# One-bank PSUM tiles in place of two-bank tiles for the last two token tiles of a decoder trunk

## The chip, the cores and the metric

The kernel runs on one core of a Trainium2 chip. The metric is device time in microseconds (us), the median of several runs. The core has five engines that work side by side, each through its own queue in order: TensorE (PE) for matmuls, VectorE (DVE) and ScalarE (ACT) for elementwise work, GpSimd (POOL), and SyncE (SP), which here only issues transfers. PE writes its results to PSUM, which is handed out in eight banks of 128 partitions by 512 float32 values. The profile shows loads of stationary operands as a row of their own (PEld).

## The reference

The model is a residual stream `x` of 512 tokens by 1024 features that passes through two layers, an attention mixer (MLA) and a gated linear attention (GLA), each followed by a squared-ReLU MLP, and a last RMSNorm. The part that matters here is the end:

```python
def sq_relu_mlp(xn, w_up, w_down):
    hid = jnp.square(jax.nn.relu(xn @ w_up))
    return hid @ w_down

for i in range(DEPTH):
    ...
    x = x + sq_relu_mlp(rms_norm(x, norm_mlp[i]), mlp_w_up[i], mlp_w_down[i])
return rms_norm(x, final_norm)
```

## The kernel before, in words

The stream is kept transposed: `xT[m]`, m = 0 to 7, is a tile of 128 features by 512 tokens. Every float32 product is done as three matmuls on parts (`mm3`, lines 110 to 112: high times high, high times low, low times high).

The MLP (`mlp`) goes over the 4096 hidden features in eight blocks of 512. `up` or `up_fast` computes a block `hid`; `down` multiplies it by its rows of `w_down` and adds the result to `xT` (line 787). `up_fast` runs seven products into two-bank PSUM tiles "z" and "y" (lines 879 and 880) and interleaves them with the `down` tiles of the block before.

The last block of the last layer is done by `down_final` instead, because the final norm follows at once. Its two halves of the tokens take different ways:

- Tokens 0 to 255 stay transposed. For m = 0 to 7 a bank "b" takes 12 matmuls of 256 columns, line 809 adds it to `xT[m]`, and `Final.add` collects squares and scaled copies. `Final.mean` (lines 1433 and 1434) sums the squares on PE, `Final.finish` computes the root on ACT and DVE, scales the eight copies (line 1443) and sends them out in four transfers (line 1444).
- Tokens 256 to 511 are two token-major tiles, t = 2 and t = 3, of 128 tokens by 1024 features. Each is two column halves, c = 0 and c = 1, and each half fills one bank with 12 matmuls of 512 columns. For t = 2 the residual is transposed by PE into a bank "b" (line 127), copied by ACT (line 824) and added by DVE (line 825). For t = 3 PE adds the residual itself, by four matmuls with the identity (line 831). `Final.row` then squares the half on ACT (line 1455), multiplies it by the gain on DVE (line 1456), and after c = 1 computes the row factor (lines 121, 1464 to 1466), scales the row (lines 1470 and 1472) and sends it out (line 1473).

PSUM is divided by `psum_layout`, which closes the current pool of tiles and opens another. There are two layouts:

```python
BANKS = {False: {"a": 2, "b": 3, "c": 3}, True: {"b": 3, "c": 1}}
```

With True, the remaining four banks are the two tiles "z" and "y", each 128 by 1024, so two banks and one tile (`two_banks`); `split_banks` returns the two halves of such a tile. Before the change `down_final` runs under True, and t = 2 takes the halves of "z", t = 3 those of "y".

The order of the work is not written out by hand. The program is traced in the order of the source, and a planner places each instruction on its engine's queue: by the order of the source, but where the next instruction would have to wait by the planner's reckoning, a later one that is ready goes ahead. It also sets the waits: an instruction that writes a tile waits for those that still read what was there, and the first instruction on a bank after a pool is closed waits for the last use of that bank in the old pool (`reuse_waits="tile"`: tile by tile).

Of the kernel before, what the change touches and what calls it, by code (L numbers as in the profile page):

```python
# [48 lines left out]
def trunk_kernel(ctx: ExitStack, tc: tile.TileContext, t_in: dict, out: bass.AP, out_row: bass.AP):  # L49
# [7 lines left out]
    def uname(s):  # L57
        count[0] += 1
        return f"{s}_{count[0]}"
# [5 lines left out]
    def psum_layout(paired):  # L65
        if psum:
            psum["es"].close()
        es = psum["es"] = ExitStack()
        psum["pool"] = es.enter_context(
            tc.tile_pool(name=uname("psum"), bufs=1, space=bass.MemoryType.PSUM, reuse_waits="tile")  # L70
        )
        psum["banks"] = BANKS[paired]

    def bank(tag):
        return psum["pool"].tile([P, 512], F32, tag=f"ps_{tag}", bufs=psum["banks"][tag], name=uname("ps"))

    def two_banks(tag):
        return psum["pool"].tile([P, 1024], F32, tag=f"ps_{tag}", bufs=1, name=uname("ps2"))

    def split_banks(tag):  # L80
        t = two_banks(tag)
        return [t[:, :512], t[:, 512:]]
# [4 lines left out]
    def tmp(shape=(P, 512), dt=F32):  # L87
        return sb.tile(list(shape), dt, tag="tmp", bufs=6, name=uname("tmp"))
# [5 lines left out]
    def both_parts():  # L94
        return sb.tile([P, 2, S], F32R, tag="set_A", bufs=8, name=uname("set"))
# [4 lines left out]
    def split(src, hi, lo, hi_eng=ACT, lo_eng=DVE, order=lambda i: i):  # L100
        if hi_eng is ACT:
            order(ACT.activation(hi, src, AF.Copy))  # L102
        else:
            hi_eng.tensor_copy(hi, src)
        lo_eng.tensor_tensor(lo, src, f(hi), ALU.subtract)  # L105

    def mm3(psum, w, x, start, stop):
        wh, wl = w
        xh, xl = x
        PE.matmul(psum, wh, xh, start=start, stop=False)  # L110
        PE.matmul(psum, wh, xl, start=False, stop=False)  # L111
        PE.matmul(psum, wl, xh, start=False, stop=stop)  # L112
# [13 lines left out]
    def tr(psum, src):  # L126
        PE.transpose(psum, src, ident[: src.shape[0], : src.shape[0]])  # L127


    def load(src, a, n):  # L130
        raw = sb.tile([P, a, n], F32, tag="wraw", bufs=2, name=uname("wraw"))
        SP.dma_start(raw, src)
        return raw
# [7 lines left out]
    def cut(pair, *idx):  # L141
        return tuple(t[idx] for t in pair)
# [601 lines left out]
    def mlp(layer, nrm, tag, nxt, final=False):  # L744
# [28 lines left out]
        def down(b, hid):  # L773
            for c in range(2):
                src = w_dn[b * FB : (b + 1) * FB, c * 512 : (c + 1) * 512].rearrange("(k p) n -> p k n", p=P)
                if c == 0 and b < NB - 1:
                    raw = fast.tile([P, 4, 512], F32, tag="raw", name=uname("raw"))
                    SP.dma_start(raw, src)
                else:
                    raw = load(src, 4, 512)  # L780
                for g in range(2):
                    w = piece(raw[:, :, g * 256 : (g + 1) * 256], 4, 256)
                    for j in range(2):
                        m = c * 4 + g * 2 + j
                        p = bank("b")
                        a_type(p, w, hid, cols=slice(j * P, (j + 1) * P))
                        DVE.tensor_tensor(xT[m], p, xT[m], ALU.add)  # L787
                        if b == NB - 1:
                            nxt.add(m, xT[m])
                        yield  # L790
# [3 lines left out]
        def down_final(b, hid):  # L794
            W = []
            for c in range(2):
                raw = load(
                    w_dn[b * FB : (b + 1) * FB, c * 512 : (c + 1) * 512].rearrange("(k p) n -> p k n", p=P), 4, 512
                )
                for k in range(4):  # L800
                    w = both_parts()
                    split(raw[:, k], w[:, 0], w[:, 1])
                    W.append((w[:, 0], w[:, 1]))
            for m in range(ND):
                p = bank("b")[:, :TH]
                for k in range(4):
                    w = cut(W[m // 4 * 4 + k], slice(None), slice(m % 4 * P, (m % 4 + 1) * P))
                    mm3(p, w, cut(hid[k], slice(None), slice(0, TH)), k == 0, k == 3)
                DVE.tensor_tensor(xT[m][:, :TH], p, xT[m][:, :TH], ALU.add)
                nxt.add(m)  # L810
            for t in (2, 3):
                tk = slice(t * P, (t + 1) * P)
                ps_ = split_banks("zy"[t % 2])
                for c in range(2):
                    for k in range(4):
                        mm3(ps_[c], cut(hid[k], slice(None), tk), W[c * 4 + k], k == 0, t == 2 and k == 3)
                        if t == 2 and c == 0 and k == 1:
                            nxt.mean()
                    if t == 2:
                        x_t = bank("b")  # L820
                        for j in range(4):
                            tr(x_t[:, j * P : (j + 1) * P], xT[c * 4 + j][:, tk])
                        y = tmp()
                        ACT.activation(y, x_t, AF.Copy)
                        DVE.tensor_tensor(y, ps_[c], y, ALU.add)
                        nxt.row(t, c, y)
                        if c == 0:
                            nxt.finish()
                    else:
                        for j in range(4):  # L830
                            PE.matmul(ps_[c][:, j * P : (j + 1) * P], xT[c * 4 + j][:, tk], ident, start=False, stop=j == 3)
                        nxt.row(t, c, ps_[c])
# [110 lines left out]
        for b in range(NB):  # L943
            if b + 1 < NB:
                tiles = down(b, hid)

                def others(n):
                    for _ in range(n):
                        next(tiles)

                hid = up_fast(b + 1, others)
                continue
            es.close()
            if final:
                down_final(b, hid)
            else:
                for _ in down(b, hid):
                    pass
# [440 lines left out]
    n_mix1 = Norm(ND, inv_d, "mix", ND)  # L1399
    psum_layout(True)  # L1400
    mlp(0, n_mlp0, "B", n_mix1)
    psum_layout(False)
    Y = gla(0, n_mix1, "B", "B")
# [71 lines left out]
    fin = Final()  # L1475
    psum_layout(True)
    mlp(1, n_mlp1, "B", fin, True)
    fin.es.close()

# [49 lines left out]
```

## Time and profile before

| | |
|---|---|
| median of 3 runs | 1104.48 us (1103.9 to 1104.51) |
| the profiled execution | 1105.92 us |
| its span, first to last instruction | 1103.5 us |
| mean granted TensorE clock | 0.995 |
| busy: PE, PEld, DVE, ACT, POOL | 99%, 83%, 78%, 50%, 4% of the span |
| PE's share of the chain that ended last | 96% |

The span is what the profile covers; the time of the execution includes about 2.4 us around it. A row of the instructions in order of time has the start in us, the duration in us, the engine, the line of the source, the operation, its output and inputs by tile names, and the shapes; "x8" merges eight instructions into one row, and a bracket at the end gives the idle time of the engine before it and the engine and line that ended it. In the list of waits, a row has who waited, for whom, the total in us, how often, and the longest. Matmuls of PE overlap: the pace is read from the starts, not from the durations.

### The profile page before, as it was taken

To read this page: it belongs to the slowest core of one execution; us is meant where nothing else is said; L and a number is where in the kernel's file an instruction comes from. 1 tells how busy PE (TensorE), PEld (TensorE's weight loads), DVE (VectorE), ACT (ScalarE), POOL (GpSimd) and SP (SyncE) were. 2 spreads that over 40 slices of the span, in tenths; PEclk is the share of its full clock that TensorE was granted. 3 is DMA by queue.
4 is the path that set the end of the run, shared out by engine and by line. 5 is a ranking of instruction groups with operands and counts; after the bars stand their busy time and mean duration, and the time that the engine had idled before them with its cause. 6 is when DMAs were issued, how large, how long until landed. Compare 5 with 4: busy or idle time off the path is not lost.

```text
span 1103.5 us, 14105 instructions
## 1 busy us (share of the span) xinstructions
PE 1090.2 (99%) x5428; PEld 918.9 (83%) x5428; DVE 856.4 (78%) x1417; ACT 546.3 (50%) x907; POOL 40.1 (4%) x72
## 2 busy tenths in 40 slices
PE   9999999999999999999999999999999999999996
PEld 7788888888888888888788888888888888888895
DVE  7789867987977977977596584478888788788773
ACT  7576654553453454454345735455444444445452
POOL 7210002000000000000000000000000000000000
PEclk9999999999999999999999999999999999999998
DMA  7312123142332332322312222232233233233122
GB/s 221 77 48 77 39 77 115 60 133 77 103 127 77 102 127 77 100 92 82 96 62 77 78 77 77 77 115 77 77 115 114 77 116 114 77 115 115 39 96 76
DMA packets 85987, 101.35 MB, mean 92 GB/s; under 512 B 7360, under 2 KB 63936, under 8 KB 85920
## 3 DMA queue, kind: packets, MB, share of 16 engines
q1 hardware_dynamic: 84112, 99.40, 28.4%
q10 hardware_dynamic: 1808, 1.05, 0.4%
q8 instruction: 42, 0.69, 0.3%
q14 instruction: 25, 0.20, 0.1%
HBM read 98.35 MB, written 2.10 MB: 91 GB/s over the span
## 4 chain that ended last, share of the span: by engine, by line
PE 96%; DVE 1%; ACT 1%; DMA 1%; issue 0%; ACTq 0%; DVEq 0%
PE ps L110 21%; PE ps L111 21%; PE ps L112 21%; PE ps L879 16%; PE ps L880 8%; PE ps L127 2%; PE ps L1155 1%; DMA wraw_ckv<-in_mla_w_in_dram 1%; PE ps L630 0%; PE ps L1226 0%; PE ps L631 0%; PE ps L629 0%; PE ps L628 0%; PE ps L627 0%; PE ps L1205 0%; DMA xT<-in_x_dram 0%
## 5 line engine op out<-in xcount | busy, mean ns | idle before, releaser
L110 PE MATMUL ps<-set,wh 128*128 128x512 f32 x776 | 304.7, 393 | 0.2 <-ACT set L237 0.2
L111 PE MATMUL ps<-set,wh 128*128 128x512 f32 x776 | 303.2, 391 | 0.8 <-DVE set L238 0.8
L112 PE MATMUL ps<-set,wl 128*128 128x512 f32 x776 | 302.8, 390 | 0.0
L102 ACT ACTIVATE wh<-wraw 128x1024 fp32r<-128x1024 f32 x139 | 147.0, 1060 | 242.0 <-PE ps L111 122.1
L105 DVE TENSOR_TENSOR wl<-wraw,wh 128x1024 fp32r<-128x1024 f32 x139 | 170.2, 1225 | 41.0 <-ACT wh L102 41.0
L110 PEld LDWEIGHTS ps<-set,wh 128*128 128x128 f32 x776 | 145.8, 188 | 31.8 <-ACT set L237 0.9
L111 PEld LDWEIGHTS ps<-set,wh 128*128 128x128 f32 x776 | 146.0, 188 | 31.4 <-DVE set L238 2.0
L112 PEld LDWEIGHTS ps<-set,wl 128*128 128x128 f32 x776 | 145.8, 188 | 30.6
L879 PE MATMUL ps<-T,wh 128*128 128x512 f32 x448 | 157.5, 391 | 0.0
L880 PE MATMUL ps<-T,wl 128*128 128x256 f32 x448 | 126.2, 282 | 0.0
L879 PE MATMUL ps<-set,wh 128*128 128x512 f32 x336 | 119.9, 397 | 0.0
L879 PEld LDWEIGHTS ps<-T,wh 128*128 128x128 f32 x448 | 84.1, 188 | 18.2
L880 PE MATMUL ps<-set,wl 128*128 128x256 f32 x336 | 94.2, 280 | 0.0
L105 DVE TENSOR_TENSOR wl<-comb,wh 128x1024 fp32r<-128x1024 f32 x42 | 51.4, 1224 | 47.2 <-ACT wh L102 46.9
L787 DVE TENSOR_TENSOR xT<-ps,xT 128x512 f32<-128x512 f32 x120 | 82.4, 687 | 6.7 <-PE ps L112 6.7
L102 ACT ACTIVATE wh<-comb 128x1024 fp32r<-128x1024 f32 x42 | 44.6, 1061 | 83.3 <-PE ps L879 80.0
L880 PEld LDWEIGHTS ps<-T,wl 128*128 128x128 f32 x448 | 84.6, 189 | 0.5
L879 PEld LDWEIGHTS ps<-set,wh 128*128 128x128 f32 x336 | 63.1, 188 | 15.1
L897 DVE TENSOR_TENSOR tmp<-ps,tmp 128x512 f32<-128x512 f32 x98 | 67.3, 686 | 1.0
L880 PEld LDWEIGHTS ps<-set,wl 128*128 128x128 f32 x336 | 63.4, 189 | 1.6
L110 PE MATMUL ps<-wh,set 128*128 128x512 f32 x144 | 59.6, 414 | 0.0
L102 ACT ACTIVATE wh<-raw 128x1024 fp32r<-128x1024 f32 x28 | 29.5, 1054 | 57.9 <-PE ps L879 55.1
(351 smaller groups left out, 1658.3 us busy)
## 6 DMA issues: line engine op xcount, KB each, us to landing
wraw<-in_mlp_w_up_dram SPq DMA_DIRECT2D x32, 1024.0 KB, 5.4
wraw<-in_mlp_w_down_dram SPq DMA_DIRECT2D x18, 1024.0 KB, 5.1
raw<-in_mlp_w_down_dram SPq DMA_DIRECT2D x14, 1024.0 KB, 5.1
wraw<-in_gla_w_in_dram SPq DMA_DIRECT2D x12, 1024.0 KB, 5.2
wraw<-in_mla_w_o_dram SPq DMA_DIRECT2D x4, 1024.0 KB, 5.0
wraw<-in_gla_w_o_dram SPq DMA_DIRECT2D x4, 1024.0 KB, 5.0
xT<-in_x_dram SPq DMA_DIRECT2D x6, 256.0 KB, 6.5
wraw<-in_mla_w_in_dram SPq DMA_DIRECT2D x3, 512.0 KB, 7.4
```

What stands on the lines that cost most here:

```text
L102: order(ACT.activation(hi, src, AF.Copy))
L105: lo_eng.tensor_tensor(lo, src, f(hi), ALU.subtract)
L110: PE.matmul(psum, wh, xh, start=start, stop=False)
L111: PE.matmul(psum, wh, xl, start=False, stop=False)
L112: PE.matmul(psum, wl, xh, start=False, stop=stop)
L127: PE.transpose(psum, src, ident[: src.shape[0], : src.shape[0]])
L787: DVE.tensor_tensor(xT[m], p, xT[m], ALU.add)
L879: PE.matmul(o.rearrange("p (h t) -> p h t", h=2), wh, x, start=start and k == 0, stop=False, skip_group_check=True)
L880: PE.matmul(o[:, :TH], wl, x[:, 0], start=False, stop=k == KH - 1, skip_group_check=True)
L897: DVE.tensor_tensor(by_tile(r), high, by_tile(r), ALU.add)
L1155: PE.matmul(p[:, t - t0], k[:, t * P : (t + 1) * P], moving[:, t], start=True, stop=True)
```

## The change

Each of the two token-major tiles takes two one-bank tiles, of tag "a" for t = 2 and of tag "c" for t = 3, in place of one two-bank tile. For that, PSUM is switched to the layout with a, b and c before `down_final`; there the b banks of the loop over m, of `Final.mean` and of the transposes come from the new pool as well. The number and the shape of all instructions stay the same.

```diff
             for t in (2, 3):
                 tk = slice(t * P, (t + 1) * P)
-                ps_ = split_banks("zy"[t % 2])
+                ps_ = [bank("ac"[t % 2]) for _ in range(2)]
                 for c in range(2):
                     for k in range(4):
                         mm3(ps_[c], cut(hid[k], slice(None), tk), W[c * 4 + k], k == 0, t == 2 and k == 3)
...
             es.close()
             if final:
+                psum_layout(False)
                 down_final(b, hid)
```

## The prediction

> **What bounds the kernel now.** I read the page's span first, then the list of what TensorE (PE) waited for over the whole run, then the waits of the last 44 us, then the two stretches around the longest one, and last the instructions in order of time.
>
> ```profile
> span 1103.5 us, 14105 instructions
> ```
>
> ```profile
> PE ps L110 <- DVE sm L1459: 3.8, 1, 3.8
> PE ps L1366 <- DVE ones L165: 1.2, 1, 1.2
> PE ps L111 <- DVE set L238: 0.8, 1, 0.8
> PE ps L630 <- ACT set L610: 0.3, 1, 0.3
> PE ps L110 <- ACT set L237: 0.2, 1, 0.2
> ```
>
> ```profile
> PEld ps L110 <- DVE tmp L825: 0.3, 1, 0.3
> PEld ps L110 <- DVE xT L787: 0.2, 1, 0.2
> ```
>
> The second fence is everything that PE waited for in 1103.5 us: it is the bound nearly everywhere, and more than half of its 6.3 us of named idle time is one wait, on VectorE (DVE), in front of a `mm3` matmul. The third fence holds two short waits of the weight loads in the same last part. So a change that only touches the final block can give about what that one wait costs, and the rest of the working is its price.
>
> ```profile
> 1085.65:1090.55 4.90, 1.05 (x10) 0.86 (x8) 4.33 (x12) 2.21 (x7) 0.00 (x0) 0.87 0.62 214
> 1090.55:1097.03 6.48, 6.47 (x20) 5.13 (x20) 0.01 (x1) 0.00 (x0) 0.00 (x0) 0.57 0.21 81
> ```
>
> ```profile
> 1084.97 0.39 PE L110 MATMUL ps<-set,set 128*128 128x512 f32 x1
> 1085.19 0.39 PE L111 MATMUL ps<-set,set 128*128 128x512 f32 x1
> 1085.42 0.39 PE L112 MATMUL ps<-set,set 128*128 128x512 f32 x1
> 1085.65 1.05 PE L831 MATMUL ps<-ident,xT 128*128 128x128 f32 x8
> 1090.55 0.80 PE L110 MATMUL ps<-set,set 128*128 128x512 f32 x1 [3.85 <-DVE sm L1459]
> 1091.14 0.63 PE L111 MATMUL ps<-set,set 128*128 128x512 f32 x1
> ...
> 1095.41 0.63 PE L112 MATMUL ps<-set,set 128*128 128x512 f32 x1
> 1095.84 1.19 PE L831 MATMUL ps<-ident,xT 128*128 128x128 f32 x8
> ```
>
> The windows show busy time of PE, weight loads, DVE, ACT and POOL, then the granted clock. In the first, PE works 1.05 of 4.90 us while DVE is busy 4.33. In the second PE is alone, DVE has 0.01 us of work, and the clock is 0.57. The rows say what the work is: the first L831 closes tile t = 3, column half c = 0 (four additions of the residual through the identity, two records each); the twelve matmuls from 1090.55 and the L831 at 1095.84 are t = 3, c = 1, the last matmuls of the program. They need only old operands (`hid`, `W`, `xT`) and their half of the two-bank tile "y". The other half is read by DVE just before:
>
> ```profile
> 1084.10 2.77 DVE L1443 TENSOR_TENSOR o<-o,rstd 128x256 f32<-128x256 f32 x8
> 1086.79 0.69 DVE L825 TENSOR_TENSOR tmp<-ps,tmp 128x512 f32<-128x512 f32 x1
> ...
> 1089.81 0.68 DVE L1456 TENSOR_TENSOR fin_row<-ps,fin_gain 128x512 f32<-128x512 f32 x1
> 1090.41 0.14 DVE L1459 TENSOR_SCALAR sm<-sm 128x1 f32<-128x1 f32 x1
> ```
>
> The L1456 at 1089.81 is `row(3, 0)`, which reads bank c = 0 of "y". It ends at 1090.49 and PE starts at 1090.55. (The list names L1459, the next small one on the same engine.) So the matmuls into one bank wait until the reader of the other bank is done, because both are one tile. The 0.3 us wait on L825 is the same pattern one tile earlier: t = 2, c = 1 waits for the read of t = 2, c = 0; there PE had work of t = 3, c = 0 put ahead, which hides it.
>
> **The change part by part.**
>
> *Tiles of their own.* No instruction is added or removed: the 16 `mm3` calls of t = 2 and 3 (48 matmuls), the transposes and the row work stay. What goes is the order "matmuls of c = 1 after the reads of c = 0", twice.
>
> (a) The 3.85 us gap. Full pace is (1085.65 − 1084.97)/3 = 0.227 us per matmul. The eight L831 records take 1.05 us, of which the last lies over what follows; c = 1 could start about 1086.54 rather than 1090.55: 4.01 us by starts, 3.85 by idle time. I take 4.0.
>
> (b) The clock behind the gap. From 1091.14 to 1095.41 there are ten steps: 0.427 us each, not 0.227. From 1090.55 to the end of the last L831 at 1097.03 it is 6.48 us; unstalled it is 12 × 0.227 + 1.05 = 3.77. Loss 2.7 us. If the clock did not recover with the gap gone, this would stay; nothing is left that stops PE, so I take all of it. The Trainium skill (TensorE: Matmul & The Clock Gate, "What's actually happening") says that the clock falls to half after about 3.4 us idle and returns after about 3.4 us of sustained work. The trace agrees on the half (0.427 against 0.227 after 3.85 us idle) but shows the slow pace for at least 4.7 us (1091.14 to 1095.84). By the page's 3.4 us the loss would be an estimated 1.7 us and the time 1098.7; the row decides for 2.7.
>
> (c) The wait on L825. Bounds 0 and 0.3 us, by its row; the matmuls put ahead of it cover nearly all, so I take 0.05.
>
> *The pool switch ahead of the final block.* `psum_layout(False)` replaces the banks z, y, b, c by a, b, c. A new tile waits for what last used its bank. In the program of the kernel before, a pool's banks follow the order in which its tags are first asked for: z 0 and 1, c 2, y 3 and 4, b 5 to 7. By that order the new b gets banks 0 to 2 (old z and c), a gets old y, c gets old b.
>
> ```profile
> 1063.73 0.28 PE L110 MATMUL ps<-set,set 128*128 128x256 f32 x1
> ...
> 1066.48 0.28 PE L112 MATMUL ps<-set,set 128*128 128x256 f32 x1
> 1066.72 0.38 PE L110 MATMUL ps<-set,set 128*128 128x256 f32 x1
> ```
>
> ```profile
> 1056.84 0.69 DVE L897 TENSOR_TENSOR tmp<-ps,tmp 128x512 f32<-128x512 f32 x1
> ...
> 1061.78 2.49 DVE L105 TENSOR_TENSOR set<-wraw,set 128x512 fp32r<-128x512 f32 x4
> 1064.19 0.68 DVE L787 TENSOR_TENSOR xT<-ps,xT 128x512 f32<-128x512 f32 x1
> ...
> 1065.99 0.68 DVE L787 TENSOR_TENSOR xT<-ps,xT 128x512 f32<-128x512 f32 x1
> ```
>
> The loop over m starts on PE at 1063.73. The last product tile (z) was read by 1057.53, so the new b waits for nothing. Before, m = 2 reuses the bank that the L787 of 1065.99 reads until 1066.67, and starts at 1066.72 instead of 1066.60: (d) 0.12 us gained. Were the new b on the old b's banks, the first tile could wait until 1064.87 or 1066.67, 1.1 to 2.9 us; that is the upper bound of this part. a and c are first written behind all eight m tiles, and the last L787 is done before m = 2 starts: nothing.
>
> *What is late next.* PE's end moves from 1097.03 by 4.0 + 2.7 + 0.05 + 0.12 = 6.87, to about 1090.16. Behind PE's end stands a fixed tail:
>
> ```profile
> 1096.75 0.28 PE L831 MATMUL ps<-ident,xT 128*128 128x128 f32 x1
> 1097.06 0.60 ACT L1455 ACTIVATE tmp<-ps 128x512 f32<-128x512 f32 x1 [7.28 <-PE ps L831]
> ...
> 1097.78 0.69 DVE L1456 TENSOR_TENSOR fin_row<-ps,fin_gain 128x512 f32<-128x512 f32 x1 [7.22 <-ACT tmp L1455]
> ...
> 1099.10 0.62 DVE L1472 TENSOR_SCALAR fin_row<-fin_row,sm 128x768 f32<-128x768 f32 x1
> ```
>
> ACT squares the bank, DVE follows 0.75 us behind PE's end, L1472 ends 2.69 us behind it, and the output transfer and closing take 1103.5 − 99.72 − 1000 = 3.8 us. All of that stays, provided DVE is free when it is needed: at 1090.16 + 0.75 = 1090.91. DVE's own queue, whose work does not shrink, ends with L1459 at 1090.55, some 0.1 us earlier with (d). The margin is only about 0.4 us: DVE takes over as the bound right behind this gain, and any lateness of it beyond 0.4 us costs one for one. The ScalarE squares of c = 0 lie ahead of that L1456 and are inside the same margin.
>
> **Sum.** 6.87 us off the span: 1103.5 to 1096.6. The profiled execution took 1105.92 us, 2.4 outside the span and 1.4 above the median of the three runs shown; I take the gain off the median: 1104.48 − 6.9 = 1097.6. Bounds from the parts: gap 3.85 to 4.0, clock 1.7 to 2.7, (c) 0 to 0.3, (d) 0 to 0.12.
>
> **The rivals.**
>
> *DVE becomes the bound and eats part.* With PE unstalled, the second transposes come behind t = 2, c = 1 instead of ahead of it, and the order of rows, `finish` and tiles on DVE may be planned anew. If the eight L1443 (2.77 us) came to stand between the last PE work and its row, or an equal wait on ScalarE did, the end moves up to 2.8 us: 1100.4. For: the 0.4 us margin, and DVE is busy 4.33 of 4.90 us in the window. Against: all its work is ready earlier, not later.
>
> *The bank switch stalls the loop over m.* First tile on an old b bank: 1.1 to 2.9 us, 1098.7 to 1100.5. Against: the order of banks above.
>
> *The switch is a barrier (slower).* If nothing of the final block could be issued until the old pool's last read at 1066.67, the eight weight splits would also start there instead of under the previous block. DVE does four in 2.49 us; m = 0 needs four, so PE would start at about 1066.67 + 0.6 + 2.5 = 1069.8, idle 6.1 us, and pay the clock of (b) again: 6.1 + 2.7 = 8.8 lost, 1106.4. It decides from a hold of about 4.2 us on. Against: the same kind of switch stands between the other blocks, and the list of PE's waits has nothing above 0.8 us there.
>
> *The change does not do what it says.* If PE's wait at 1090.55 had another cause than the shared tile, nothing moves: 1104.5. Against: two waits of the same form, and no other late operand.
>
> **How the numbers follow.** Forecast 0.70 (own range 1097.0 to 1098.7), DVE 0.14, bank stall 0.08, no effect 0.04, barrier 0.04. Two thousandths, 2.2 us, is about what this measurement can tell from no change. The first three are faster (0.92); no effect, and the barrier at its smaller prices, are the same (0.05); the barrier at its full price or above, slower (0.03). The range runs from 1096.8, the sum with the bounds in full and the runs' spread of 0.6, to 1100.4, the end of the DVE case.
>
> **What would show it.** Right: no PE idle above 0.5 us between 1063 and the end; the last twelve L110 to L112 rows at 0.23 us; PE's last L831 ending about 6.9 us earlier; the tail behind it still 6.4 us. Wrong: a DVE wait in front of the last matmuls again; the last L1456 starting more than 0.8 us behind PE's end (DVE case); an idle stretch on PE in front of the first 256-column matmul (bank stall or barrier); a pace of 0.43 us anywhere behind it.

## The result, and the profile after

| | before | after |
|---|---|---|
| median | 1104.19 us (1103.21 to 1104.51, 4 runs) | 1097.85 us (1097.64 to 1098.16, 4 runs) |
| span of the profiled execution | 1103.5 us | 1096.1 us |

The ratio is 0.9944, 95% interval [0.9927, 0.9962]: 6.3 us less, 0.6%. The forecast was 1097.6 with a range of 1096.8 to 1100.4. A second set of five runs on another occasion gave 1097.51 against 1103.81 us, ratio 0.9942 [0.9928, 0.9955].

All that PE waited for in the whole span of the changed kernel (who waits, for whom, total us, times, longest us). Line numbers behind line 955 are one higher than before:

```profile
PE ps L1367 <- DVE ones L165: 1.2, 1, 1.2
PE ps L111 <- DVE set L238: 0.8, 1, 0.8
PE ps L630 <- ACT set L610: 0.3, 1, 0.3
PE ps L1156 <- ACT q L1163: 0.2, 1, 0.2
```

The 3.8 us in front of `mm3` are gone, and nothing has taken their place. The instructions of PE from the end of t = 3, c = 0 on:

```profile
1084.90 1.05 PE L831 MATMUL ps<-ident,xT 128*128 128x128 f32 x8
1085.71 0.48 PE L110 MATMUL ps<-set,set 128*128 128x512 f32 x1
1086.03 0.39 PE L111 MATMUL ps<-set,set 128*128 128x512 f32 x1
...
1088.32 0.39 PE L112 MATMUL ps<-set,set 128*128 128x512 f32 x1
1088.55 1.05 PE L831 MATMUL ps<-ident,xT 128*128 128x128 f32 x8
```

The last twelve matmuls start 0.81 us behind the start of the identity additions, with no idle time in brackets, and go on at (1088.32 − 1086.03)/10 = 0.229 us each. The windows (busy time of PE, weight loads, DVE, ACT, POOL; granted clock; transfers) show the same:

```profile
1084.90:1089.60 4.70, 4.70 (x29) 4.01 (x27) 4.17 (x13) 1.65 (x5) 0.00 (x0) 1.00 0.68 236
1089.60:1096.10 6.50, 0.00 (x1) 0.00 (x0) 1.76 (x5) 1.69 (x5) 0.00 (x0) 0.71 0.39 152
```

PE's last stretch, from the identity additions of c = 0 to its end, took 11.38 us before (1085.65 to 1097.03); it takes 4.70, all of it busy and at full clock. The tail behind PE's end is 6.50 us; it was 6.47. PE stayed the bound. DVE in the same stretch:

```profile
1083.38 0.69 DVE L825 TENSOR_TENSOR tmp<-ps,tmp 128x512 f32<-128x512 f32 x1
1083.98 2.76 DVE L1444 TENSOR_TENSOR o<-o,rstd 128x256 f32<-128x256 f32 x8
...
1089.11 0.14 DVE L1460 TENSOR_SCALAR sm<-sm 128x1 f32<-128x1 f32 x1
1090.36 0.69 DVE L1457 TENSOR_TENSOR fin_row<-ps,fin_gain 128x512 f32<-128x512 f32 x1 [1.10 <-ACT tmp L1456]
```

The L825 of t = 2, c = 1 now stands ahead of the eight scalings (it stood behind them, at 1086.79), and DVE is idle for 1.10 us before the last L1457, waiting for ACT, which waited for PE. PE's order changed with it: the four transposes of t = 2, c = 1 now stand behind that half's twelve matmuls, at 1081.69. Before, they and five matmuls of t = 3, c = 0 stood ahead of the twelve, which waited for the L825 of c = 0. Outside the last 70 or so instructions of each engine both programs issue the same operations in the same order.

### The profile page after: what moved, and what is told of

The parts are those of the page before. It is cut to its first block, busy times and chain, and to the rows that moved or that the text cites. A ratio compares the mean times of both kernels' runs of the same rounds, so it can differ in the third digit from the quotient of the medians.

```text
span 1096.1 us, 14102 instructions
## 1 busy us (share of the span) xinstructions
PE 1086.7 (99%) x5428; PEld 917.0 (84%) x5428; DVE 857.2 (78%) x1417; ACT 546.6 (50%) x907; POOL 39.7 (4%) x72
## 3 DMA queue, kind: packets, MB, share of 16 engines
q10 hardware_dynamic: 1808, 1.05, 0.3%
## 4 chain that ended last, share of the span: by engine, by line
PE 97%; DVE 1%; DMA 1%; ACT 1%; issue 0%; ACTq 0%; DVEq 0%
PE ps L111 21%; PE ps L110 21%; PE ps L112 21%; PE ps L879 16%; PE ps L880 9%; PE ps L127 2%; PE ps L1156 1%; DMA wraw_ckv<-in_mla_w_in_dram 1%; PE ps L1227 0%; PE ps L630 0%; PE ps L631 0%; PE ps L628 0%; PE ps L629 0%; PE ps L627 0%; PE ps L1206 0%; DMA xT<-in_x_dram 0%
## 5 line engine op out<-in xcount | busy, mean ns | idle before, releaser
L787 DVE TENSOR_TENSOR xT<-ps,xT 128x512 f32<-128x512 f32 x120 | 82.5, 688 | 7.1 <-PE ps L112 7.1
```

## The experiments

Theory A: the two banks of one tile are guarded together, so the matmuls of t = 3, c = 1 waited for the reader of c = 0; the idle time and the half clock behind it are the whole gain. Rival B: the fresh banks of the pool switch bring a good part. Rival C: it takes both tiles, by a new order of the tail. Rival D: the half pace of the last matmuls had another cause than the gap. Each kernel was compared with the kernel before on the same chip.

### The switch alone

```diff
 (changed kernel)
-                ps_ = [bank("ac"[t % 2]) for _ in range(2)]
+                ps_ = split_banks("zy"[t % 2])
```

> The pool switch alone: the final block runs in the layout with a, b and c, but t = 2 and t = 3 keep the two-bank tiles z and y (the pool has room for b, z and y). Theory A (the shared tile is the cost): the wait of about 4 us in front of the last twelve matmuls and their pace of 0.43 us both stay; the time is that of before, 1104.2, at most 0.2 us less for the m = 2 step. Rival B (the fresh banks of the loop over m bring a good part of the gain): 1099 to 1101, with the m loop ending earlier. Barrier rival: PE idle ahead of the first 256-column matmul.

1104.34 us against 1104.62, ratio 0.9997 [0.9988, 1.0007]: no change. PE in its profile:

```profile
1084.89 1.05 PE L831 MATMUL ps<-ident,xT 128*128 128x128 f32 x8
1089.82 0.59 PE L110 MATMUL ps<-set,set 128*128 128x512 f32 x1 [3.87 <-DVE sm L1460]
1090.20 0.63 PE L111 MATMUL ps<-set,set 128*128 128x512 f32 x1
...
1093.57 0.39 PE L110 MATMUL ps<-set,set 128*128 128x512 f32 x1
1093.80 0.39 PE L111 MATMUL ps<-set,set 128*128 128x512 f32 x1
```

The gap is there, 3.87 us. The half pace is there too, but ends by 1093.57, where the profiled execution of before kept it to its last matmul at 1095.41. The loop over m starts at 1063.22 and takes 11.51 us, with no wait of PE ahead of it. Rival B falls, and so do the barrier and the bank stall: the switch costs and gives nothing.

### Only t = 3

```diff
 (changed kernel)
-                ps_ = [bank("ac"[t % 2]) for _ in range(2)]
+                ps_ = split_banks("z") if t == 2 else [bank("c"), bank("c")]
```

> Only t = 3 gets one-bank tiles; t = 2 keeps the two-bank tile z and its wait on L825. Theory A: the whole gain is the wait of t = 3, c = 1; the last matmuls start right behind the identity additions of t = 3, c = 0 at full pace; 1097.9, within 0.4 us of the changed kernel. Rival C (the order of the whole tail, with both tiles freed, is what brings it): part of the gain is missing, 1099 to 1102.

1098.00 against 1104.62, ratio 0.9942 [0.9927, 0.9957]: all of the gain. Rival C falls. What differs from the changed kernel is the slack of DVE before the last product:

```profile
1090.38 0.69 DVE L1457 TENSOR_TENSOR fin_row<-ps,fin_gain 128x512 f32<-128x512 f32 x1 [0.54 <-ACT tmp L1456]
```

It is 0.54 us, not 1.10. Freeing t = 2 gives DVE slack and no time.

### Only t = 2

```diff
 (changed kernel)
-                ps_ = [bank("ac"[t % 2]) for _ in range(2)]
+                ps_ = [bank("a"), bank("a")] if t == 2 else split_banks("y")
```

> Only t = 2 gets one-bank tiles; t = 3 keeps the two-bank tile y. Theory A: the wait in front of the last twelve matmuls stays, 2.5 to 4 us of idle time (the read of t = 3, c = 0 on DVE may come up to 1.3 us earlier, since the DVE add of t = 2, c = 1 can move ahead of the eight scalings), and the half pace with it; 1102.5 to 1104.2. Rival C: half the gain, about 1101.

1102.86 against 1104.62, ratio 0.9987 [0.9977, 0.9996]: about 1.5 us less, inside the range of theory A.

```profile
1084.71 1.05 PE L831 MATMUL ps<-ident,xT 128*128 128x128 f32 x8
1089.08 0.79 PE L110 MATMUL ps<-set,set 128*128 128x512 f32 x1 [3.31 <-DVE sm L1460]
1089.67 0.63 PE L111 MATMUL ps<-set,set 128*128 128x512 f32 x1
...
1092.53 0.39 PE L112 MATMUL ps<-set,set 128*128 128x512 f32 x1
```

The wait stays but is 0.5 us shorter, because the reader that it waits for comes earlier on DVE; the half pace stays too, up to about 1092.5. So the length of the gap was DVE's backlog, not a fixed cost: the second half waits as long as the other work in front of the reader takes. The gap accounts for 0.5 of the 1.5 us. For the rest there is only a hint: three of these ten runs have a granted clock of 0.995, against ten of the nineteen of the kernel before.

### No switch

```diff
 (kernel before)
                 ps_ = split_banks("zy"[t % 2])
+                if t == 3:
+                    ps_[1] = bank("c")
```

> No pool switch: the kernel before, with t = 3, c = 1 in the one bank c that its layout has and everything else in z, y and b as before. Theory A: all of the gain without the switch, 1097.9 (within 0.4 us), PE gap gone. Rival B (the switch is needed): 1101 to 1104.

1098.03 against 1104.62, ratio 0.9942 [0.9925, 0.9958]: all of the gain with one bank moved and no switch. This also tests step (d), the 0.12 us at m = 2, since the loop over m keeps the old banks here. The end of t = 3, c = 0, then the first matmul of the loop and the first behind it, and ACT's wait for the weights of the last block:

```profile
1085.36 1.05 PE L833 MATMUL ps<-ident,xT 128*128 128x128 f32 x8
1086.17 0.48 PE L110 MATMUL ps<-set,set 128*128 128x512 f32 x1
```

```profile
1063.65 0.28 PE L110 MATMUL ps<-set,set 128*128 128x256 f32 x1
...
1075.16 0.40 PE L110 MATMUL ps<-set,set 128*128 128x512 f32 x1
```

```profile
1052.51 0.63 ACT L102 ACTIVATE set<-wraw 128x512 fp32r<-128x512 f32 x1 [1.39 <-DMA wraw<-in_mlp_w_down_dram]
```

The gap is gone: the last matmuls start 0.81 us behind the additions, as in the changed kernel. The loop takes 11.51 us on the old banks, as in the changed kernel (1063.34 to 1074.85) and not 11.72 as in the profiled execution of before. That execution had this line instead:

```profile
1054.96 1.16 ACT L102 ACTIVATE set<-wraw 128x512 fp32r<-128x512 f32 x2 [3.76 <-DMA wraw<-in_mlp_w_down_dram]
```

The weights landed later there, ACT and DVE were late by some 2.5 us, and the L787 that m = 2 waited for was late with them.

### The gap filled with work

```diff
 (kernel before, behind nxt.row(t, c, ps_[c]) of t = 3)
+                        if c == 0:
+                            scrap = bank("c")
+                            for _ in range(16):
+                                PE.matmul(scrap, W[0][0][:, :P], W[0][0], start=True, stop=True)
```

> The kernel before, with 16 extra matmuls of 512 columns into an unused bank (tag c), queued on PE between t = 3, c = 0 and c = 1, so that PE is busy through its wait (16 x 0.227 = 3.6 us of the 4.0); their result is not used. The wait of c = 1 on DVE's read stays. Theory A (the half pace comes from the idle gap): the last twelve matmuls run at 0.227 us, 2.7 us less than before: 1101.7. Rival D (the half pace has another cause, such as DVE or the transfers working beside it): pace 0.43 and the time of before, 1104.4.

1102.05 against 1104.21, ratio 0.9980 [0.9971, 0.9988]: 2.2 us less, with the wait as before.

```profile
1084.96 1.05 PE L831 MATMUL ps<-ident,xT 128*128 128x128 f32 x8
1085.77 3.91 PE L836 MATMUL ps<-set 128*128 128x512 f32 x16
1089.86 0.50 PE L110 MATMUL ps<-set,set 128*128 128x512 f32 x1 [0.19 <-DVE sm L1463]
1090.20 0.40 PE L111 MATMUL ps<-set,set 128*128 128x512 f32 x1
1090.44 0.39 PE L112 MATMUL ps<-set,set 128*128 128x512 f32 x1
```

The last matmuls start at the same moment as with the gap (1089.82 in the switch-alone kernel) and run at 0.23 us. Their window, with the columns as above:

```profile
1089.86:1093.77 3.91, 3.90 (x20) 3.22 (x20) 0.01 (x1) 0.00 (x0) 0.00 (x0) 1.00 0.34 134
```

Rival D falls: as in that window of before (0.57, 81 GB/s over 6.48 us), DVE does 0.01 us of work beside them and the transfers move 0.52 MB, yet the clock is full. This splits the gain: 2.2 us were the clock, and the remaining 4.2 us (6.34 − 2.16, each against its own kernel before) the idle time. The traces give 4.1 for the latter: from the additions to the last matmuls it is 4.90 us here (1084.96 to 1089.86) and 0.81 in the changed kernel.

### Half of it filled

The same with `range(8)`.

> The same with 8 extra matmuls (1.8 us), which leaves some 2.2 us of idle PE in front of the last twelve; their result is not used. If a gap of 2.2 us is too short to lower the clock: 1101.7, as with 16. If the cost of the clock goes with the length of the gap: about 1103, between before and 16. If any gap lowers it: 1104.4.

1103.80 against 1104.21, ratio 0.9990 [0.9981, 0.9999]. The median says little here: the eleven runs fall into two groups, five at 1101.9 to 1102.4 and six at 1103.8 to 1104.5. The profiled one is of the first:

```profile
1085.78 2.09 PE L836 MATMUL ps<-set 128*128 128x512 f32 x8
1089.91 0.50 PE L110 MATMUL ps<-set,set 128*128 128x512 f32 x1 [2.04 <-DVE sm L1463]
1090.24 0.39 PE L111 MATMUL ps<-set,set 128*128 128x512 f32 x1
```

A gap of 2.04 us, and full pace behind it. None of the three expectations holds for all runs. Five of the six slower runs have longer spans too, 1101.7 to 1102.5 us against 1099.9 to 1100.5 in the first group; the sixth (1104.22) has a span of 1100.8, and most of its excess lies outside the span. That the five pay the clock is argued from the size of the step (about 2 us of span) and from their granted clock (0.997 to 0.998, against 0.998 to 0.999 in the first group); no profile of such a run was taken.

### How far DVE is from being the bound

```diff
 (changed kernel, behind nxt.row(t, c, ps_[c]) of t = 3)
+                        if c == 0:
+                            yh = nxt.y[:, :512]
+                            for _ in range(4):
+                                DVE.tensor_tensor(yh, yh, yh, ALU.max)
```

> The changed kernel with four extra DVE instructions of 128x512 behind row(3, 0) (a maximum of the row with itself, about 0.6 us each, 2.4 us in all). It measures how far DVE is from being the bound behind PE's end. By the trace of the changed kernel (DVE idle 1.10 us ahead of the last L1457): 2.4 - 1.1 = 1.3 us slower than the changed kernel, 1099.2. By the prediction's margin of 0.4 us: 2.0 slower, 1099.9. If DVE has no part in the end: 1097.9.

1099.42 against 1104.21, ratio 0.9954 [0.9940, 0.9967]: 1.6 us above the changed kernel's 1097.85, near the 1.3 us that its trace gave and not the 2.0 of the prediction's margin.

```profile
1089.68 1.42 DVE L836 TENSOR_TENSOR fin_row<-fin_row 128x512 f32<-128x512 f32 x2
1091.02 0.68 DVE L1461 TENSOR_TENSOR fin_row<-ps,fin_gain 128x512 f32<-128x512 f32 x1
1091.62 0.68 DVE L836 TENSOR_TENSOR fin_row<-fin_row 128x512 f32<-128x512 f32 x1
...
1093.39 0.62 DVE L1477 TENSOR_SCALAR fin_row<-fin_row,sm 128x768 f32<-128x768 f32 x1
```

PE's last additions start at 1088.97 and end 1.05 us later, at 1090.02. The last scaling starts 3.37 us behind that end; in the changed kernel it is 2.08 us (1089.60 to 1091.68). The difference, 1.29 us, is the 2.4 us of added work less 1.1 us of slack. PE itself ended 0.42 us later in this execution.

### Less work on PE, now that PE sets the end

```diff
 (changed kernel)
-  mm3(..., k == 0, t == 2 and k == 3)
-  if t == 2 and c == 0 and k == 1:   # nxt.mean()
+  mm3(..., k == 0, (t == 2 or c == 0) and k == 3)
+  if t == 2 and c == 0 and k == 2:   # nxt.mean()
-  if t == 2:                         # residual by transposes, ACT copy, DVE add
+  if t == 2 or c == 0:
-  if c == 0:                         # nxt.finish()
+  if t == 2 and c == 0:
...
-  if m < ND - 1:
-      DVE.tensor_tensor(self.acc, self.acc, self.sq, ALU.add)
+  DVE.tensor_tensor(self.acc, self.acc, self.sq, ALU.add)
...
-  PE.matmul(self.ms, inv_d, self.acc, start=True, stop=False)
-  PE.matmul(self.ms, inv_d, self.sq, start=False, stop=True)
+  PE.matmul(self.ms, inv_d, self.acc, start=True, stop=True)
```

> The changed kernel with less work on PE in the tail: t = 3, c = 0 takes its residual by transposes, an ACT copy and a DVE add, as t = 2 does (PE 0.5 us less, DVE one more L825 of 0.6), and Final.mean is one float32 matmul in place of two (PE 0.43 less, one DVE add of 0.43 more). PE's end moves by about 0.95 us; DVE, with a margin of 1.1 us less 0.95 less 0.6, comes to be the bound and gives back about 0.45: 1097.4. If PE alone sets the end: 1096.9. If DVE's order in the tail gets worse: 1098 or above.

1096.88 against 1104.21, ratio 0.9932 [0.9920, 0.9945].

```profile
1089.32 0.69 DVE L1455 TENSOR_TENSOR fin_row<-ps,fin_gain 128x512 f32<-128x512 f32 x1 [0.43 <-ACT tmp L1454]
```

DVE still waits 0.43 us before its last product, for ACT, which reads PE's last bank; so PE alone sets the end. I had expected DVE to give back 0.45 us. But with the shorter mean its work starts earlier too (the L825 of t = 2, c = 1 at 1082.74, against 1083.38), and from there to its last small operation of t = 3, c = 0 it takes 6.14 us against 5.87: the added L825 costs 0.27 and not 0.6. To set it beside the changed kernel, both were run again on one chip:

> The changed kernel once more, beside the version with less work on PE on the same chip: 1097.9, with a spread below 1 us, since no idle gap is left that could lower the clock.

> The version with less work on PE in the tail, on the same chip as the changed kernel. If the 1.0 us between the two medians is real and PE alone sets the end: 1096.9, all runs below those of the changed kernel. If it was the chip: no difference.

The changed kernel took 1097.51 us (1097.27 to 1098.30), this one 1096.89 (1096.52 to 1097.16), five runs each that do not overlap: 0.6 us, less than the 1.0 of the separate runs and the 0.87 by which PE's work behind the loop over m shrank in the two traces (1074.66 to 1088.54, against 1074.85 to 1089.60). It beats both kernels, by little.

## Why the prediction was right, point by point

**The place and the cause.** Right. One reader of one half of a two-bank tile held the matmuls into the other half; the kernel with one bank moved and no switch gets the whole gain.

**(a) The gap, 4.0 us.** Right: 4.2 us by the difference between filling it and removing it, 4.1 by the two traces.

**(b) The clock, 2.7 us.** The term that was furthest off: 2.2 us [1.3 to 3.2, from the interval of the ratio], inside the bounds of 1.7 to 2.7 given but not at the end taken, which the interval still holds. The row was right for its execution, and that was one of the longer ones. Over 49 executions of the kernel before, 22 have a granted clock of 0.995 and spans of 1102.2 to 1103.7 us, and 27 have 0.996 to 0.998 and spans of 1101.2 to 1102.3; the profiled one (0.995, 1103.5) is of the first group. On the chip of the filled kernel (median span 1100.3) the 21 runs of before have median spans of 1102.8 in the first group and 1102.0 in the second: 2.5 and 1.7 us more. The windows in which the clock stood at half, in the profile of before (with the window ahead of it) and in that of the switch-alone kernel, show one gap with two prices:

```profile
1085.65:1089.28 3.63, 1.05 (x9) 0.86 (x7) 3.06 (x10) 1.71 (x7) 0.00 (x0) 1.00 0.83 289
1089.28:1096.10 6.82, 5.55 (x14) 4.41 (x15) 1.27 (x3) 0.50 (x2) 0.00 (x0) 0.50 0.20 77
```

```profile
1090.08:1093.50 3.42, 3.42 (x9) 2.65 (x9) 0.00 (x0) 0.00 (x0) 0.00 (x0) 0.50 0.37 145
```

The first stretch is twice the second. Its first 1.27 us lie in the gap and the other 5.55 cost about half their length, 2.8 us; the 3.42 of the second cost about 1.7. That this is what divides the 49 executions is argued from their clocks and spans; one of each kind was profiled. In the switch-alone kernel the slow pace lasts from 1090.08 to 1093.50, 3.4 us. There the trace agrees with the one window of about 3.4 us that the Trainium skill states (TensorE: Matmul & The Clock Gate, "What's actually happening"); the prediction had set its estimate aside for a single trace. (Its own terms with 1.7 us for the clock give 1098.6, not the 1098.7 written there.)

**(c) The wait on L825, 0.05 us.** Right that it is worth nothing by itself. What the step missed is that freeing t = 2 moves the DVE add of c = 1 ahead of eight scalings, 2.8 us. The prediction had the new order of the transposes and of DVE among its rivals, as a danger; it came, and it gave DVE slack.

**(d) The bank of m = 2, 0.12 us.** Wrong as a term of every run. The loop over m takes 11.51 us on old and new banks alike; the wait in the profile of before came from weights that landed late in that execution. No profile shows the new banks with weights as late as that.

**The tail and DVE's margin.** The tail stayed, 6.50 against 6.47 us, and DVE did not become the bound. The margin was put at 0.4 us; it is 1.10, and 0.54 where only t = 3 is freed. The 0.4 assumed that DVE's order would not change; (c) says why it did.

**The sum.** The forecast took 6.87 us off 1104.48; the medians differ by 6.34. The clock was taken 0.5 us too large, (d) 0.12 and (c) 0.05 too large, and the gap 0.2 too small. That the forecast is nevertheless within 0.3 us is in part luck: a fourth run lowered the median of before by 0.29, which offsets about half of that 0.53. The spans of the two profiled executions differ by more, 7.4 us, because the profiled execution of before was 1.4 us above its median: 6.7 us lie in PE's last stretch, and 0.75 ahead of it (the loop over m starts 0.39 us earlier and is 0.21 shorter, and what follows up to 1084.90 is 0.15 shorter).

## What to carry to other kernels

When the halves of a two-bank tile are filled and read at different times, look at what guards them. Here the planner guards the tile, so the second half waits for the reader of the first, and the price is whatever stands in front of that reader in its queue, unless PE has other work to put ahead (as for t = 2, which cost nothing). When PE has a named wait on an engine that is busy with other things, ask first whether the data is really shared. Before a short term is read off one profile, its neighbours (a late transfer, a clock dip) must be seen in a second one.

## What the runs showed of the hardware that was not expected

The cost of one idle gap of PE is not one number. With a gap of 3.85 us in its profile the kernel before ran from 1103.0 to 1106.5 us in 19 runs on one chip (spans of 1101.2 to 1103.3); without it, four runs of the kernel with only t = 3 freed on the same chip lie within 0.5 us. The profiles show the clock at half for 6.82 us in one execution and for 3.42 in another. In the profile of before the clock fell 2.6 us behind PE's last addition (1086.70 to 1089.28), and with the gap of 2.04 us no fall is seen before the end of PE's work. Even so, a gap of 2.04 us seems enough to cost some 1.8 us in about half of the runs (five or six of eleven), where the Trainium skill's page above speaks of an idle window of about 3.4 us; the trace taken with that gap shows no loss, so this rests on the times alone.
